# A decoder layer in float32: the sixth pair of up products as seven products of halves, its weight sums kept in DRAM

## The chip, the cores and the metric

One core of a Trainium2 chip runs the whole kernel. The metric is device microseconds of one execution; a kernel is run several times, and the median counts. A profile is taken of one execution more, and its trace gives each instruction's engine, start and length. The engines are PE (matmuls; its weight loads are listed as PEld), DVE and ACT (element by element), POOL, and SP, which here only issues DMAs, in the order in which they stand.

## What is computed

The reference is one post-norm decoder layer on 512 tokens of 1024 features, all in float32: forgetting attention with 16 heads, a gated MLP with a causal convolution over three tokens, and a gated embedding.

```
proj = x @ w_in;  q, k, v, f_logit = split(proj)
c = cumsum(log_sigmoid(f_logit + b_f))
s = q k^T / 8 + c_i - c_j  (causal);  mix = softmax(s) v @ w_out
x = layer_norm(alpha * x + mix)
u, g = split(x @ w_up);  g = causal_dwconv(g, conv_w, conv_b)
x = layer_norm(alpha * x + (gelu(g) * u) @ w_down)
x = x + sigmoid(x @ w_gate + b_gate) * (p @ w_proj)
```

The MLP is 2816 wide: u and g are 22 blocks of 128 features each, and two neighbouring blocks f = 2j, 2j + 1 are a pair j, from 0 to 10.

## The kernel before, in words

**Products.** Every operand is cut in two parts of PE's float32r type, a high part (names ending in h or hi) and the low rest (l or lo), and each product is three matmuls: high by high, high by low, low by high (`three`, line 147). A weight unit is a tile of 128 x 1024 numbers. The class `Weights` (line 64) holds the list of units in the order of their use, loads them from DRAM on SP into four buffers (tag `raw`, `load_to`, line 81; in the MLP every fifth unit goes into a spare tile, `side`), and cuts them (`cut_to`, line 105): ACT writes `whi` (line 123), DVE writes `wlo` (line 129). There are five `whi`/`wlo` buffers, so a unit is cut up to four units before its use, when the product five units back is done.

**Order.** V is projected in three groups of heads (`value_rows`, line 399), the first together with the first Q/K block. Then a loop over h takes head h's scores (`scores`), the projection of a later Q/K block (`project`), the transposes of head h-1's probabilities (`turn`) and head h-2's values (`values`), and at the end the out projection. Here a scheduler decides how the instructions of each engine stand. The MLP follows in four parts of three pairs (the last of two). Each part's up products (`up`, line 763, or `up_step`, line 810) have the down products of the part before laid in (`down`, line 884; chains named x, y, z, added into y by DVE, `add_half`, line 674). From line 945 on the order of DVE and ACT is the order in which the code is written (`manual_schedule`); PE's is still the scheduler's.

**Plain pairs.** `up` makes u or g of one block f as eight chained products of 128 x 512, 24 matmuls. `conv` (line 773) reads g from PSUM, and `product` multiplies with u from PSUM into the tile E.

**Pairs in UP_PAIRS** (line 34). Of the 2 x 2 blocks (two features' blocks by two halves of the 1024 inputs, and two halves of the tokens) seven products of halves are made in place of eight, by Strassen's scheme in Winograd's form. `up_step` does it in four steps, each for g and for u: st 0 makes two products of 128 x 256 per k, st 1 and st 2 two each, st 3 one. Between the steps ACT copies halves of PSUM into E and DVE adds. The weights enter as sums of blocks (`up_units`, line 238). For pairs not kept, DVE makes the sums as the unit is used (`t12`, `t3`, `t4`).

**Kept pairs** (`KEPT`, line 36). Their sums are made early, while DVE has time, and stored in DRAM as an item `kept[j, q]` for each of u and g. An item is made by `keep_load` (line 455: two loads of 512 KB into `ka`, one buffer, and `kb`, one of the four `raw` buffers) and by `keep_sums` (line 469: four subtractions of 128 x 512 on DVE); the next `keep_load` first stores the item (two DMAs) and then loads the next. Before, this is called ahead of V's second group, between the groups, and in the head loop at h = 0 and every even h from 4 to 14.

**Down operands.** The pair's result E (one buffer) becomes the operands of the down products by `operand_sums` (four additions on DVE) and `operand_parts` (names a, b, s with the pair's number, three copies on ACT and three subtractions on DVE). For a pair in `APART` (line 40) this work for the pair before it is written behind the pair's own first step, and E is taken anew after it; else it is written right behind the pair before.

Of the kernel before, what the change touches and what calls it, by code (L numbers as in the profile page):

```python
# [24 lines left out]
KD = D // P  # L25
# [5 lines left out]

CHUNKS = (None, (1,) * 12, (1,) * 12, (2, 1) * 4)

UP_PAIRS = (2, 3, 4, 6, 7, 9)

KEPT = (3, 4, 6, 7)

DMA_PAIRS = (1, 2)

APART = (2, 3, 4, 7)  # L40
HALF = S // 2
ALPHA = 2.0 ** 0.25
EPS = 1e-5
# [99 lines left out]
def trunk_layer(ctx: ExitStack, tc: tile.TileContext, xT, x2d, pT, w0, wqk, wv1, wv2, bf, wo, wup, cwb,  # L143
# [142 lines left out]
    for part in range(4):  # L286
# [3 lines left out]
        for i in range(2 * len(fs)):  # L290
            f, q = fs[i // 2], i % 2
            j, n = f // 2, i % 4
            if j in UP_PAIRS:
                stages = up_units(j)
# [101 lines left out]

    proj = {}

    def value_rows(n):
        h0, nh = V_HEADS[n]  # L400
        w = VF if n == 0 else wv[n].shape[1]
        pv = [bank(f"pv{t}_{n}") for t in range(NT)]
# [3 lines left out]
        for k in range(KD):  # L406
# [21 lines left out]
            if n == 0 and k == 0:  # L428
                with tc.issue_after(cut_first):
                    cut_x(1)  # L430
        for t in range(NT):
            if n == 0:
                logits[t] = fl_all[:, t * H:t * H + H]
                nc.scalar.activation(logits[t], pv[t][:, nh * DH:w], AF.Copy)
            v = V[:, t, h0:h0 + nh]
            p3 = pv[t][:, :nh * DH].rearrange("p (h d) -> p h d", d=DH)
            nc.scalar.activation(v[:, :, 0, :], p3, AF.Copy)
            nc.vector.tensor_sub(v[:, :, 1, :], p3, v[:, :, 0, :].bitcast(F32))
# [30 lines left out]
    def keep_sums():  # L469

        if in_work:
# [9 lines left out]
            behind.close()  # L481
            made.append((to, ab))


    stacks, probs = {}, {}

# [139 lines left out]

    stack(0)
    keep_load()
    value_rows(1)
    stack(1)  # L630
    keep_sums()
    keep_load()
    value_rows(2)
    for h in range(H + 2):
        m, s = divmod(h, 2)
        if h == 2:
            project(2, 0)
        if h < H:
            scores(h)

            if s == 0 and h != 2:
                keep_sums()
                keep_load()
        if m + 1 < KD and h != 2:
            project(m + 1, s)
        for k in OUT_FIRST.get(h, ()):
            out_first(k)
        if s == 1 and h + 1 < H:
            stack(h + 1)
        if 1 <= h < H + 1:  # L650
            turn(h - 1)
        if h >= 2:
            values(h - 2)
        if s == 1 and h + 1 < H:
            stack(h + 2)
        if h == H:
            y = base.tile([P, NT, D], F32, tag="xh", name="y")
            for t in range(NT):
                nc.sync.dma_start(y[:, t, :], x2d[t * P:(t + 1) * P, :])
# [271 lines left out]
    for part in range(4):  # L931
# [7 lines left out]
        for f in range(6 * part, min(6 * part + 6, NF)):  # L939
# [39 lines left out]
            else:  # L979
# [3 lines left out]
                n = 4 * (j - 3 * part) + 2 * q  # L983
# [245 lines left out]
```

## Time and profile before

| | |
|---|---|
| median of 3 runs | 646.31 us (645.73 to 647.5) |
| profiled execution | 646.34 us, its span 644.4 us |
| granted clock of PE | 0.999 |
| busy: PE, DVE, ACT, POOL | 638.1, 532.5, 384.2, 127.8 us |
| HBM read, written | 107.72 MB, 18.87 MB |

The time of an execution holds the span of its trace, from the first to the last instruction, and 1.94 us around it. PE counts as busy from a matmul's start to its modelled end, so its share alone does not tell how fast it goes: the chain that ended last, read in order of time, tells where PE went on and where it waited. The attention with the first half of its out projection takes the first 220 us or so; the MLP's up products run from 247 to 565 us.

### The profile page before, as it was taken

The numbers are of one execution on the slowest core, as the hardware profiler recorded it, in microseconds if no ns is written. First come the engines' busy times: TensorE is split into PE (matmuls) and PEld (weight loads), VectorE is DVE, ScalarE is ACT, GpSimd is POOL, SyncE is SP. The second block draws the span as 40 slices with busy tenths as digits, with TensorE's granted clock in tenths as the row PEclk, the third lists the DMA queues.
The fourth block names the chain that finished last, engine by engine and source line by source line (L and its number), as shares of the span: only waits on it lengthen the run. The fifth ranks groups of instructions, "written<-read, shape, count | busy, mean of one in ns | idle before, by whom it ended". The sixth has DMA issues, their size and how long they took to land.

```text
span 644.4 us, 10100 instructions
## 1 busy us (share of the span) xinstructions
PE 638.1 (99%) x3635; PEld 562.4 (87%) x3635; DVE 532.5 (83%) x866; ACT 384.2 (60%) x685; POOL 127.8 (20%) x147
## 2 busy tenths in 40 slices
PE   8999999999999999999999999999999999999997
PEld 7999888888888889989999988999988998888886
DVE  6674779988888599857899987889797998699997
ACT  6463777877775316945657563647555455336872
POOL 2000554454456043110000010101011001002001
PEclk9999999999999999999999999999999999999999
DMA  8863625454588387684776839665746764772632
GB/s 287 273 213 131 205 83 179 160 187 155 184 263 322 129 257 216 140 213 145 212 221 159 231 121 246 194 206 149 240 132 199 192 217 116 168 272 65 228 109 98
DMA packets 49441, 121.08 MB, mean 188 GB/s; under 512 B 4912, under 2 KB 7984, under 8 KB 49392
## 3 DMA queue, kind: packets, MB, share of 16 engines
q1 hardware_dynamic: 44448, 107.20, 49.8%
q0 software_dynamic: 4800, 13.11, 10.9%
q8 instruction: 28, 0.46, 0.3%
q14 instruction: 21, 0.17, 0.1%
q10 hardware_dynamic: 144, 0.14, 0.1%
HBM read 107.72 MB, written 18.87 MB: 196 GB/s over the span
## 4 chain that ended last, share of the span: by engine, by line
PE 96%; DVE 2%; DMA 1%; issue 0%; ACT 0%; SPq 0%; DVEq 0%
PE g L152 18%; PE u L152 18%; PE pp L152 13%; PE x L152 8%; PE pv L152 7%; PE pl L152 7%; PE z L152 4%; PE r L152 3%; PE ap L152 3%; PE o L581 3%; PE t L568 2%; PE ao L152 2%; PE y L152 2%; PE s L531 2%; PE s L533 2%; PE p L152 1%
## 5 line engine op out<-in xcount | busy, mean ns | idle before, releaser
L123 ACT ACTIVATE whi<-raw 128x1024 fp32r<-128x1024 f32 (+4 forms) x139 | 128.6, 929 | 91.5 <-PE pv L152 15.3
L129 DVE TENSOR_TENSOR wlo<-raw,whi 128x1024 fp32r<-128x1024 f32 (+5 forms) x134 | 140.3, 1055 | 28.3 <-ACT whi L123 27.7
L555 POOL TENSOR_SCALAR pr<-pr,rl 128x128 f32<-128x128 f32 (+1 forms) x64 | 75.5, 1197 | 128.6 <-DVE rl L551 128.6
L281 POOL COPY neghalf<-neghalf 128x1 f32<-128x1 f32 x16 | 9.0, 563 | 247.0 <-ACT neghalf L280 247.0
L152 PE MATMUL g<-x1h,whi 128*128 128x256 f32 (+1 forms) x168 | 54.7, 325 | 0.0
L152 PE MATMUL g<-x1l,whi 128*128 128x256 f32 (+1 forms) x168 | 54.4, 324 | 0.0
L152 PE MATMUL g<-x1h,wlo 128*128 128x256 f32 (+1 forms) x168 | 54.4, 324 | 0.0
L152 PE MATMUL u<-x1l,whi 128*128 128x256 f32 (+1 forms) x160 | 52.9, 331 | 0.0
L152 PE MATMUL u<-x1h,wlo 128*128 128x256 f32 (+1 forms) x160 | 52.9, 331 | 0.0
L152 PE MATMUL u<-x1h,whi 128*128 128x256 f32 (+1 forms) x160 | 52.9, 331 | 0.0
L152 PE MATMUL pp<-xh,wlo 128*128 128x512 f32 (+1 forms) x130 | 50.7, 390 | 0.0
L152 PE MATMUL pp<-xh,whi 128*128 128x512 f32 (+1 forms) x130 | 50.4, 388 | 0.0
L152 PE MATMUL pp<-xl,whi 128*128 128x512 f32 (+1 forms) x130 | 50.4, 387 | 0.0
L547 ACT ACTIVATE pr<-s,nm 128x128 f32<-128x128 f32 (+1 forms) x64 | 33.6, 528 | 9.2 <-DVE nm L543 9.0
L152 PEld LDWEIGHTS g<-x1h,whi 128*128 128x128 f32 x168 | 31.9, 190 | 3.4 <-issue 0.7
L152 PEld LDWEIGHTS g<-x1l,whi 128*128 128x128 f32 x168 | 31.9, 190 | 2.7
L152 PEld LDWEIGHTS g<-x1h,wlo 128*128 128x128 f32 x168 | 31.9, 190 | 2.5
L152 PEld LDWEIGHTS u<-x1h,whi 128*128 128x128 f32 x160 | 30.4, 190 | 3.0
L152 PEld LDWEIGHTS u<-x1l,whi 128*128 128x128 f32 x160 | 30.4, 190 | 3.0
L152 PEld LDWEIGHTS u<-x1h,wlo 128*128 128x128 f32 x160 | 30.4, 190 | 2.8
L123 ACT ACTIVATE whi<-side 128x512 fp32r<-128x512 f32 (+1 forms) x33 | 25.5, 782 | 10.7 <-DVE wlo L129 1.8
L152 PE MATMUL pv<-whi,xh 128*128 128x384 f32 (+1 forms) x96 | 31.0, 322 | 0.7 <-ACT whi L123 0.6
(636 smaller groups left out, 1869.4 us busy)
## 6 DMA issues: line engine op xcount, KB each, us to landing
raw<-wup SPq DMA_DIRECT2D x34, 512.0 KB, 9.6
raw<-wdn SPq DMA_DIRECT2D x23, 512.0 KB, 6.2
raw<-wqk SPq DMA_DIRECT2D x14, 512.0 KB, 4.0
ka<-wup SPq DMA_DIRECT2D x8, 512.0 KB
kb<-wup SPq DMA_DIRECT2D x8, 512.0 KB
kept<-kb SPq DMA_DIRECT2D x8, 512.0 KB, 3.2
kept<-ka SPq DMA_DIRECT2D x8, 512.0 KB
raw<-wo SPq DMA_DIRECT2D x8, 512.0 KB, 4.2
```

The source lines that it names most:

```text
L123: self.nc.scalar.activation(hi[:, c:e], piece, AF.Copy)
L129: self.nc.vector.tensor_sub(lo[:, c:e], piece, hi[:, c:e].bitcast(F32))
L152: nc.tensor.matmul(ps, lhsT, rhs, start=start and n == 0, stop=stop and n == 2, skip_group_check=on)
L281: with tc.issue_after(nc.gpsimd.tensor_copy(small[:, m + 32:m + 33], small[:, m:m + 1]).ins):
L531: nc.tensor.matmul(ps[:, :n], QA[:, q], KA[:, :n], start=True, stop=False)
L533: nc.tensor.matmul(ps[:, :n], qb[0:68, q], kb[0:68, :n], start=False, stop=True)
L547: nc.scalar.activation(pr[:, off:off + w], ps[:, :w], AF.Exp, bias=nm[:, i:i + 1], scale=-1.0, accum_out=ls[:, i:i + 1])
L555: nc.gpsimd.tensor_scalar_mul(pr[:, off:off + w], pr[:, off:off + w], rl[:, i:i + 1])
L568: nc.tensor.transpose(ps[:, w:w + P], pr[:, o:o + P], ident)
L581: nc.tensor.matmul(ps[:, q0:], V[:, j, h], p[:, o:o + w], start=j == 0 and n == 0, stop=j == NT - 1 and n == 1)
```

## The change

The sixth pair (j = 5), plain before, joins `UP_PAIRS` and `KEPT`, so its four plain products become seven products of halves for g and for u, and two more items are kept (ten in place of eight). Pairs 5 and 6 join `APART`. The two more items are made by calls of `keep_sums` and `keep_load` (now together `keep`) in the middle of V's second and of V's third group; the calls in the head loop are as many as before, and each now works on an item two further in the list.

```
-UP_PAIRS = (2, 3, 4, 6, 7, 9)
-KEPT = (3, 4, 6, 7)
+UP_PAIRS = (2, 3, 4, 5, 6, 7, 9)
+KEPT = (3, 4, 5, 6, 7)
...
-APART = (2, 3, 4, 7)
+APART = (2, 3, 4, 5, 6, 7)
...
-    def value_rows(n):
+    def value_rows(n, amid=None):
...
+            if amid is not None and k == KD // 2:
+                amid()
...
+    def keep():
+        keep_sums()
+        keep_load()
...
     stack(0)
     keep_load()
-    value_rows(1)
+    value_rows(1, keep)
     stack(1)
-    keep_sums()
-    keep_load()
-    value_rows(2)
+    keep()
+    value_rows(2, keep)
```

On SP, between V's second group and head 0's scores, the queue of before has the Q/K weights of the first heads (raw18 to raw22; QA1 is a row of the second head's operands) and one load of an item's `kb`:

```order
L511 DMA QA1_573<-QA1_573 64x512
L93 DMA raw18_631<-wqk 128x1024
L93 DMA raw19_661<-wqk 128x1024
L93 DMA raw20_691<-wqk 128x1024
L466 DMA kb4_0_761<-wup 128x1024
L93 DMA raw21_768<-wqk 128x1024
L93 DMA raw22_828<-wqk 128x1024
```

After it, in the same place (kept3_1 and kept4_0 are the second and third items in DRAM):

```order
L93 DMA raw17_613<-wqk 128x1024
L462 DMA kept3_1_64<-kb3_1_532 128x1024
L462 DMA kept3_1_64<-ka3_1_531 128x1024
L93 DMA raw18_643<-wqk 128x1024
L93 DMA raw19_673<-wqk 128x1024
L468 DMA ka4_0_601<-wup 128x1024
L468 DMA kb4_1_694<-wup 128x1024
L93 DMA raw20_713<-wqk 128x1024
L462 DMA kept4_0_65<-kb4_0_602 128x1024
L468 DMA kb5_0_783<-wup 128x1024
L462 DMA kept4_0_65<-ka4_0_601 128x1024
L93 DMA raw21_790<-wqk 128x1024
```

The stores of two items and the loads of two more now stand between the Q/K weights. raw21 takes the buffer that the third item's `kb` had, so its load waits for that item's store; before, it waited for the cut of raw19. On ACT the high part of raw21 is cut ahead of head 0's exponentials, before as after.

On DVE, from the last product of the fifth pair (E4 is its E, a4l and so on the low parts of its down operands, x, y and z the down products' sums), before:

```order
L786 TENSOR_TENSOR E4_3898<-a8_4131,E4_3898 128x512
L873 TENSOR_TENSOR E4_3898<-E4_3898 128x256
L874 TENSOR_TENSOR E4_3898<-E4_3898 128x256
L875 TENSOR_TENSOR E4_3898<-E4_3898 128x256
L876 TENSOR_TENSOR E4_3898<-E4_3898 128x256
L882 TENSOR_TENSOR a4l_4140<-E4_3898,a4h_4139 128x512
L882 TENSOR_TENSOR b4l_4142<-E4_3898,b4h_4141 128x256
L882 TENSOR_TENSOR s4l_4144<-E4_3898,s4h_4143 128x1024
L223 TENSOR_TENSOR raw84_4092<-raw84_4092,side_2724 128x512
L129 TENSOR_TENSOR wlo83_4162<-raw83_4044,whi83_4161 128x1024
L129 TENSOR_TENSOR wlo84_4192<-raw84_4092,whi84_4191 128x512
L679 TENSOR_TENSOR y_2402<-y_2402,x00_3474 128x512
```

And in the change, from the same product (g10 is the sixth pair's g in PSUM, `side` here the place of its first step's half):

```order
L790 TENSOR_TENSOR E4_3920<-a8_4154,E4_3920 128x512
L129 TENSOR_TENSOR wlo83_4173<-raw83_4066,whi83_4172 128x1024
L844 TENSOR_TENSOR side_2746<-g10_4171,side_2746 128x256
L223 TENSOR_TENSOR side_2746<-side_2746 128x512
L129 TENSOR_TENSOR wlo84_4208<-raw84_4114,whi84_4207 128x1024
L683 TENSOR_TENSOR y_2424<-y_2424,x00_3496 128x512
L683 TENSOR_TENSOR y_2424<-y_2424,x01_3497 128x512
L683 TENSOR_TENSOR y_2424<-y_2424,z00_3494 128x512
L683 TENSOR_TENSOR y_2424<-y_2424,z01_3495 128x512
L129 TENSOR_TENSOR wlo85_4231<-side_2746,whi85_4230 128x512
L877 TENSOR_TENSOR E4_3920<-E4_3920 128x256
L878 TENSOR_TENSOR E4_3920<-E4_3920 128x256
```

The fifth pair's sums and low parts have moved behind the sixth pair's first cuts and the four y adds; the two more sums, a join for u, and then a4l, b4l and s4l follow. The sixth pair's new E can be written by ACT only when s4l has been made. On PE the six matmuls of a down product (unit 82) now stand in the middle of the second step's g product, and those of unit 85 behind it.

More of the change, by code (lines that the diff above doesn't have):

```diff
@@ L641, in trunk_layer @@
             if s == 0 and h != 2:
-                keep_sums()
-                keep_load()
+                keep()
         if m + 1 < KD and h != 2:
```

## The prediction

> **What bounds the kernel now.** I read the page first (busy times, then the shares of the chain that ended last), then the chain of waits in order of time around the sixth pair, the busy times by stage, and last the timelines of single engines at the two places the change touches. From the page:
>
> ```profile
> span 644.4 us, 10100 instructions
> PE 638.1 (99%) x3635; PEld 562.4 (87%) x3635; DVE 532.5 (83%) x866; ACT 384.2 (60%) x685; POOL 127.8 (20%) x147
> PE 96%; DVE 2%; DMA 1%; issue 0%; ACT 0%; SPq 0%; DVEq 0%
> ```
>
> PE carries 96% of the chain, so a change pays what it takes off PE less what it makes PE wait. The chain in order of time (start, length, what), from the end of the fifth pair (j = 4) over the sixth (j = 5) to the start of the seventh; the last row is a plain half step of the fifth pair, for comparison:
>
> ```profile
> 373.33 1.44 PE u L152 x12
> 374.77 5.47 PE g L152 x24
> 380.23 1.36 PE x L152 x6
> 381.59 1.36 PE z L152 x6
> 382.95 5.44 PE u L152 x24
> 388.39 2.27 PE x L152 x10
> 390.66 5.69 PE g L152 x24
> 396.35 0.45 PE x L152 x2
> 396.80 5.44 PE u L152 x24
> 402.24 1.36 PE x L152 x6
> ...
> 343.65 2.88 PE g L152 x24
> ```
>
> The four pieces of 24 between 374.77 and 402.24 are the sixth pair's plain products, 128x512 each; the x and z pieces between them are down products that are laid in. No piece is followed by a gap. The second reading is how full DVE is in that stretch (columns: PE, PEld, DVE, ACT, POOL busy, clock, DMA share, GB/s):
>
> ```profile
> 340.77:371.89 31.12, 31.12 (x219) 29.16 (x218) 28.92 (x41) 19.76 (x35) 2.43 (x4) 1.00 0.72 199
> 371.89:403.60 31.71, 31.71 (x153) 26.45 (x152) 25.11 (x37) 16.17 (x25) 3.07 (x4) 1.00 0.66 184
> 403.60:431.84 28.24, 28.24 (x194) 26.28 (x194) 23.76 (x35) 14.81 (x27) 2.91 (x4) 1.00 0.67 198
> ```
>
> A kept pair (first row, j = 4) runs DVE at 93% and PE still never waits; the sixth pair (second row) has been the rest in between, with 6.6 us of DVE free.
>
> **The products themselves.** Removed: 4 x 24 matmuls of 128x512 at 5.44 us per 24, 21.76 us. Added: seven products of halves for u and for g, 3 x 24 + 12 matmuls of 128x256 each, at 2.88 per 24 and 1.44 per 12 (rows at 343.65 and 373.33): 2 x (3 x 2.88 + 1.44) = 20.16. All of it is on the path: -1.60 us. The down products between them stay. One plain piece, at 390.66, takes 5.69 where its like takes 5.44: the third product follows the plain conv of the first, and the 0.25 us goes with the plain form (bounds 0 and -0.25; I take -0.25, since a kept pair has no product that waits for the conv of its own pair's first half).
>
> A page of the Trainium skill speaks on the first term: "TensorE: Matmul & The Clock Gate", section "Wait — 56ns, not 53.3ns?", has back-to-back warm matmuls start N ÷ 2.4 GHz plus about 2.5 ns apart, 109 ns for 256 columns and 216 for 512. By it the pair would fall from 20.7 to 18.4 us, an estimate of -2.4 instead of -1.60. The trace does not agree: 2.88 over 24 is 120 ns and 5.44 over 24 is 227 ns, so here a half costs 53% of a whole, not 51%.
>
> **DVE and ACT in the sixth pair.** A kept pair cuts seven 1024-units' worth of weights where a plain one cuts four, and joins the products on DVE. From the groups of the fifth pair (columns: count, busy, mean ns, idle before):
>
> ```profile
> L129 DVE TENSOR_TENSOR wlo<-raw,whi 128x1024 fp32r<-128x1024 f32 x8 | 9.8, 1222 | 1.2 <-ACT whi L123 1.2
> L129 DVE TENSOR_TENSOR wlo<-raw,whi 128x512 fp32r<-128x512 f32 x3 | 2.0, 690 | 0.4 <-ACT whi L123 0.2
> L851 DVE TENSOR_TENSOR E<-g,E 128x512 f32<-128x512 f32 x1 | 0.7, 693 | 0.4 <-PE g L152 0.4
> L840 DVE TENSOR_TENSOR side<-g,side 128x256 f32<-128x256 f32 x1 | 0.4, 418 | 0.0
> ```
>
> Cuts: 6 x 1.22 + 2 x 0.69 - 4 x 1.22 = 3.82; joins: 2 x 0.42 + 2 x 0.69 = 2.2; 6.0 us more on DVE. Put into the second window that is 25.11 + 6.0 = 31.1 against 31.71 - 1.6 = 30.1 us: DVE overdrawn by 1.0 us there, with 28.24 - 23.76 = 4.5 us free in the next. So PE will wait somewhere in the pair, and the question is how long. The place is the third step: its g product needs two ACT copies into the new E tile, and those wait until DVE has read the last of the old one. The fifth pair shows that chain without a wait (product of the pair before, first cut after it, two y adds, last low part, second copy), and the last row is the sixth pair's own start:
>
> ```profile
> 348.55 0.69 DVE L786 TENSOR_TENSOR E<-a,E 128x512 f32<-128x512 f32 x1 [0.16 <-ACT a L785]
> 356.80 1.22 DVE L882 TENSOR_TENSOR s3l<-E,s3h 128x1024 fp32r<-128x1024 f32 x1
> 358.86 0.37 ACT L845 ACTIVATE E<-g 128x256 f32<-128x256 f32 x1
> 386.56 1.28 DVE L679 TENSOR_TENSOR y<-y,x 128x512 f32<-128x512 f32 x2
> 379.66 0.69 DVE L786 TENSOR_TENSOR E<-a,E 128x512 f32<-128x512 f32 x1 [0.16 <-ACT a L785]
> ```
>
> In the fifth pair the product ends at 349.24, the last low part at 358.02 (8.8 later), the copy at 359.23 (1.2 more). In the sixth the same list has four y adds (2.5) and a 512 cut (0.7) more and a 1024 cut (1.2) less, so 10.8 us: from 380.35 to 391.1, and the copy ends at 392.3. PE arrives there after 4 x 2.88 of halves and 2.72 + 1.36 + 1.36 of down products: 374.77 + 16.96 = 391.73. It waits 0.55 us. The down product before it (the first of those with six matmuls) needs the first y add: 380.35 + 0.1 + 1.22 + 0.42 + 0.69 + 1.22 (cut, join, subtraction, cut) + 0.7 = 384.7, and PE is there at 374.77 + 2.5 x 2.88 + 2.72 = 384.7: nothing to spare, nothing lost. So +0.55, bounds 0 and 2.0 (every link later by the 1.0 us of overdraft, twice). The rest of the overdraft meets the pair's last steps: bounds 0 and +1.0, taken +0.2, nearest to the free 4.5 us behind it. The seventh pair's operands of the sixth are now made in its own first steps, as the eighth pair has it already, plus two ACT copies of 0.4 us with ACT at 14.81 of 28.24: nothing. The pair reads 1.5 MB more by DMA in a stretch at share 0.66; the fifth reads as much at 0.72 and waits for nothing: nothing.
>
> **The two items made beside V.** Each is two loads, four sums, two stores of 512 KB. The sums (all eight items have the same lengths) and the stage they go into:
>
> ```profile
> L477 DVE TENSOR_TENSOR ka<-kb,ka x8: 685/686/692, 25.3 to 194.0; 128x512 f32<-128x512 f32 x8
> 52.00:56.00 4.00, 4.00 (x25) 4.00 (x24) 1.02 (x2) 1.06 (x1) 0.00 (x0) 1.00 0.38 131
> 56.00:60.00 4.00, 4.00 (x25) 4.00 (x24) 1.11 (x2) 1.06 (x1) 0.00 (x0) 1.00 0.37 129
> ```
>
> 2 x 4 x 0.7 = 5.6 us of sums, with 2.9 us of every 4 free on DVE there, and PE never waiting: the sums cost nothing. The transfers are another matter, since SP issues in order and takes them ahead of the later Q/K weights. The rows of that chain (a wqk group from 44.16 holds three issues, one from 57.10 two; then ACT and POOL of head 0, and PE's transposes of it; last the median times to landing):
>
> ```profile
> 42.08 0.96 DVE L129 TENSOR_TENSOR wlo<-raw,whi 128x768 fp32r<-128x768 f32 x1
> 44.16 4.93 SPq L93 DMA_DIRECT2D raw<-wqk  x3
> 57.10 4.44 SPq L93 DMA_DIRECT2D raw<-wqk  x2
> 63.06 1.05 ACT L123 ACTIVATE whi<-raw 128x1024 fp32r<-128x1024 f32 x1
> 64.51 1.28 ACT L547 ACT_TABLE_LOAD   x1
> 65.81 0.37 ACT L547 ACTIVATE pr<-s,nm 128x128 f32<-128x128 f32 x1
> 67.74 0.21 ACT L547 ACTIVATION_READ_ACCUMULATOR pr<-s,nm 128x1 f32 x1
> 68.27 4.81 POOL L555 TENSOR_SCALAR pr<-pr,rl 128x128 f32<-128x128 f32 x4 [63.41 <-DVE rl L551]
> 76.52 1.25 PE L568 MATMUL t<-ident,pr 128*128 128x128 f32 x10
> raw<-wqk SPq DMA_DIRECT2D x14, 512.0 KB, 4.0
> kept<-kb SPq DMA_DIRECT2D x8, 512.0 KB, 3.2
> ```
>
> The load of raw21 goes out at 57.10 now. In the change it takes the buffer of the third item's kb, so it waits for that item's store: the second item's last sum ends at about 42.08 + 2.8 (sums) + 0.7 + 2 x 0.95 (what stands between them) = 47.5; its store lands 3.2 later, 50.7; the third item's load takes 4.0 and, behind five other transfers of 512 KB, about 1.5 more, 56.2; three sums, 58.3; store 3.2, 61.5; then raw21, 4.0 and some queueing, about 66. The high part of raw21 is cut on ACT ahead of head 0's exponentials, and from its landing it is 1.05 + 1.3 + 2.1 + 0.3 + 4.8 = 9.6 us to the last scaled row, which PE needs at about 76.5. So the landing may be as late as 66.9 before PE waits; beyond that every us costs one. I take +0.2, bounds 0 and +5 (below). A gain is excluded: PE has no gap there to close.
>
> **Sum.** -1.60 - 0.25 + 0.55 + 0.2 + 0.2 = -0.9 us on the profiled execution's 646.34 (span 644.4 and 1.94 around it), which stands at the median of the runs, 646.31: 645.4.
>
> **Rivals.** (1) The chain of transfers beside V decides: four legs stand in a row (store, load, store, load), and if each takes 1.5 us more than I gave it, raw21 lands near 72 and PE stands 5 us at head 0's transposes: 650.5, slower. For it: only 0.9 us are to spare, and the stage's bytes double (4 MB more in some 30 us, beside 130 GB/s). Against it: the same legs land in 3.2 to 4.0 us today. It decides from a landing at 66.9. (2) DVE's overdraft costs more than 0.75 us, each of three waits (y add, copy, last step) 0.7 to 1 us: about +2.0 in place of 0.75 and nothing gained, 646.3 to 647.5. For it: 93% in the pair before and no rest in between. Against it: the 4.5 us behind. (3) No wait at all: 646.34 - 1.85 = 644.5. For it: PE shows no wait in the kept pair before it. (4) A product of halves costs half a whole: 24 in 2.72 us, the pair in 19.04, -2.72 in place of -1.60: 644.3. The rows at 343.65 and 373.33 speak against it, since they are that very product in the pair before. By the page of the Trainium skill named above it would be 644.6, an estimate. That the products are not made as said is excluded: the changed program has 72 matmuls more on PE, 168 for 96.
>
> **Chances.** About 0.3% of this kernel, 1.94 us, is what a measurement of it can tell from no change: faster is below 644.4, slower above 648.25. Forecast (644.9 to 646.2) 0.43, all within. Rival 2: 0.22, of it 0.02 slower. Rival 3: 0.20, of it 0.11 faster, since it sits on the bound and the runs shown spread by 0.6 below their median. Rival 1: 0.13, of it 0.11 slower. Rival 4: 0.02, faster. That makes 0.13 faster, 0.74 within, 0.13 slower. The range reaches down to rival 3 less 0.4 of that spread, 644.1, and up into rival 1, 648.9, which leaves out some 0.07 below and 0.08 above.
>
> **What would show it.** In the profile after: 24 matmuls of 128x256 in 2.88 us all through the pair, 168 of them; a wait of PE of about half a us at the third step, released by ACT's copy; DVE near 100% in the stretch of the sixth pair and freer in the seventh; head 0's exponentials starting 1.5 to 3 us later against the scores, and its transposes still at 76.5. The forecast is wrong if head 0's transposes move, if the pair from 374.77 takes more than 28.8 us, or if PE's time changes in the attention or behind the seventh pair.

## The result, and the profile after

The changed kernel takes 650.71 us (median of 9 runs, 648.54 to 653.61) against 646.55 us (median of 9, 645.73 to 647.5): 1.0064 of the time, 95% interval 1.0045 to 1.0084. The forecast of 645.4 is wrong in sign, and the time lies above the range. It is close to the 650.5 of the first rival, and the experiments show that rival's chain of transfers at work; they also show that the pair itself gains nothing (1.0011 of the time with the pair alone). The profiled execution took 652.2 us. Its page:

```profile
span 650.3 us, 10314 instructions
PE 638.8 (98%) x3707; PEld 564.9 (87%) x3707; DVE 542.5 (83%) x882; ACT 391.2 (60%) x703; POOL 127.8 (20%) x147
PE 80%; DMA 7%; DVE 7%; ACT 2%; issue 2%; POOL 1%; SPq 0%; DVEq 0%; ACTq 0%
```

PE's share of the chain fell from 96% to 80%; DMA and DVE hold 7% each. PE's busy time rose by only 0.7 us (638.1 to 638.8) where the span rose by 5.9 (644.4 to 650.3). So the time came as waits, and the chain says where. First the stage beside V and head 0, in order of time (start, length, what):

```profile
47.71 4.82 DMA kept<-ka
...
52.54 6.83 DMA ka<-wup
...
61.67 2.90 DMA kept<-kb
...
64.58 5.69 DMA raw<-wqk
...
70.35 1.06 ACT whi L123
...
71.43 1.28 ACT L553
...
72.72 2.16 ACT pr L553 x8
...
75.19 4.93 POOL pr L561 x4
...
80.16 0.98 PE t L574 x7
```

These are the legs of the prediction's chain, store, load, store, load, and then the cut of unit 21 (the cut at 70.35), the exponentials, the scaling and the transposes of head 0. Each leg is in the place where it was expected, and three of the four are longer. PE's waits in this stage, from its timeline:

```profile
65.03 0.50 PE L152 MATMUL pp<-xh,wlo 128*128 128x512 f32 x1 [0.61 <-DVE V L440]
...
73.23 0.50 PE L537 MATMUL s<-KA,QA 128*128 128x512 f32 x1 [1.80 <-ACT pr L553]
...
90.37 0.50 PE L587 MATMUL o<-PTh,V 128*128 128x512 f32 x1 [1.35 <-ACT pr L553]
```

The same product of head 0 with V in the kernel before:

```profile
85.38 0.50 PE L581 MATMUL o<-PTh,V 128*128 128x512 f32 x1
```

It starts 5.0 us late now, and 5.4 us of lateness reach the sixth pair. The first of the three waits is for V's last rows, which DVE adds behind the third item's sums, and those waited for their load. The second, 1.80 us, is for head 0's exponentials, at head 1's scores; at head 0's transposes themselves PE waits only 0.22 us more. In the sixth pair the chain reads:

```profile
395.05 0.92 DVE s4l L886
...
396.19 0.83 DVE wlo L129
...
397.32 0.68 DVE raw L223
...
399.06 0.69 DVE wlo L129
...
399.77 8.35 DMA raw<-wup
...
408.22 0.04 ACT whi L123
...
409.18 0.37 ACT E L859
...
409.60 2.41 PE g L152 x18
```

DVE ends the operand parts of the pair before at 396, then cuts weights that have been waiting for it. Only with these cuts do buffers come free, so the load that PE will need leaves at 399.77. It lands 8.35 us later; ACT cuts that unit and only then copies a finished result out of PSUM, and PE, which needs that bank for the seventh pair's first product, has waited 1.27 us.

In the table, which serves all the experiments too, the three columns behind the ratio are read from each profiled execution's timeline: the start of head 0's product with V, the start of the sixth pair, and the time from there to the start of the ninth (three pairs). Where nothing was changed ahead of it, the first of these columns lies between 85.2 and 85.9, which is its spread; `exps_h1_ordered`'s profiled execution is an exception, since it lost some 3 us at its start, with half the clock between 10 and 14 us.

| kernel | median us | ratio, 95% interval | head 0 x V | sixth pair | three pairs |
|---|---|---|---|---|---|
| before | 646.55 | 1 | 85.38 | 374.60 | 91.07 |
| changed | 650.71 | 1.0064, 1.0045 to 1.0084 | 90.37 | 380.00 | 91.93 |
| items_only | 650.48 | 1.0056, 1.0044 to 1.0069 | 88.63 | 378.03 | 91.05 |
| pair_only | 647.24 | 1.0011, 1.0002 to 1.0019 | 85.90 | 375.21 | 91.44 |
| small_transfers | 648.40 | 1.0030, 1.0020 to 1.0040 | 87.06 | 376.73 | 92.38 |
| no_sums | 650.54 | 1.0052, 1.0032 to 1.0071 | 87.74 | 377.38 | 93.40 |
| exps_first | 647.39 | 1.0018, 1.0005 to 1.0030 | 85.74 | 375.10 | 91.10 |
| exps_h1 | 647.09 | 1.0011, 1.0000 to 1.0022 | 85.92 | 375.20 | 91.30 |
| heads_items | 656.09 | 1.0131, 1.0110 to 1.0153 | 85.39 | 382.10 | 91.34 |
| heads_pool | 660.33 | 1.0218, 1.0204 to 1.0232 | 85.69 | 388.69 | 92.35 |
| late_items | 651.62 | 1.0079, 1.0065 to 1.0092 | 85.88 | 380.89 | 91.06 |
| late_ordered | 654.12 | 1.0106, 1.0082 to 1.0130 | 85.42 | 383.38 | 91.76 |
| copies_first | 650.57 | 1.0061, 1.0047 to 1.0075 | 89.75 | 379.13 | 91.19 |
| pair_relief | 645.06 | 0.9981, 0.9972 to 0.9989 | 85.72 | 374.98 | 90.19 |
| pair_ordered | 646.70 | 1.0007, 0.9996 to 1.0018 | 85.21 | 374.52 | 91.78 |
| exps_pool | 651.13 | 1.0069, 1.0052 to 1.0087 | 87.81 | 377.08 | 93.92 |
| exps_pool_h1 | 649.39 | 1.0052, 1.0035 to 1.0070 | 84.77 | 374.59 | 93.92 |
| exps_h1_ordered | 647.11 | 0.9999, 0.9988 to 1.0011 | 88.38 | 377.61 | 91.61 |

The ratio is against the runs of the kernel before on the same chip, whose medians lay between 646.33 and 646.62. It need not equal the quotient of the medians; the intervals decide.

### The profile page after: what moved, and what is told of

Its sections match the earlier page's. It is cut to its first block, busy times and chain, and to the rows that moved or that the text cites. A ratio compares the mean times of both kernels' runs of the same rounds, so it can differ in the third digit from the quotient of the medians.

```text
span 650.3 us, 10314 instructions
## 1 busy us (share of the span) xinstructions
PE 638.8 (98%) x3707; PEld 564.9 (87%) x3707; DVE 542.5 (83%) x882; ACT 391.2 (60%) x703; POOL 127.8 (20%) x147
## 4 chain that ended last, share of the span: by engine, by line
PE 80%; DMA 7%; DVE 7%; ACT 2%; issue 2%; POOL 1%; SPq 0%; DVEq 0%; ACTq 0%
PE g L152 16%; PE u L152 16%; PE pp L152 10%; PE x L152 7%; PE pl L152 7%; PE z L152 4%; PE r L152 3%; PE ap L152 3%; PE o L587 3%; PE ao L152 2%; PE t L574 2%; PE y L152 2%; PE s L537 1%; DVE wlo L129 1%; PE s L539 1%
## 5 line engine op out<-in xcount | busy, mean ns | idle before, releaser
L123 ACT ACTIVATE whi<-raw 128x1024 fp32r<-128x1024 f32 (+4 forms) x142 | 131.1, 929 | 101.2 <-DMA raw<-wqk 17.7
L129 DVE TENSOR_TENSOR wlo<-raw,whi 128x1024 fp32r<-128x1024 f32 (+5 forms) x137 | 143.5, 1055 | 27.8 <-ACT whi L123 27.0
L561 POOL TENSOR_SCALAR pr<-pr,rl 128x128 f32<-128x128 f32 (+1 forms) x64 | 75.7, 1200 | 133.6 <-DVE rl L557 133.6
L152 PE MATMUL g<-x1h,whi 128*128 128x256 f32 (+1 forms) x164 | 51.8, 316 | 1.3 <-ACT E L859 1.3
L152 PE MATMUL g<-x1l,whi 128*128 128x256 f32 (+1 forms) x164 | 51.6, 315 | 0.0
L152 PE MATMUL g<-x1h,wlo 128*128 128x256 f32 (+1 forms) x164 | 51.5, 314 | 0.0
L152 PE MATMUL u<-x1h,whi 128*128 128x256 f32 (+1 forms) x156 | 50.1, 321 | 0.3 <-DVE E L855 0.3
L152 PE MATMUL u<-x1l,whi 128*128 128x256 f32 (+1 forms) x156 | 50.1, 321 | 0.0
L152 PE MATMUL u<-x1h,wlo 128*128 128x256 f32 (+1 forms) x156 | 50.1, 321 | 0.0
L152 PE MATMUL g<-xsh,whi 128*128 128x256 f32 x112 | 31.7, 283 | 0.1
L152 PE MATMUL u<-xsl,whi 128*128 128x256 f32 x112 | 31.7, 283 | 0.0
```

What stands on the lines that cost most here:

```text
L123: self.nc.scalar.activation(hi[:, c:e], piece, AF.Copy)
L129: self.nc.vector.tensor_sub(lo[:, c:e], piece, hi[:, c:e].bitcast(F32))
L152: nc.tensor.matmul(ps, lhsT, rhs, start=start and n == 0, stop=stop and n == 2, skip_group_check=on)
L561: nc.gpsimd.tensor_scalar_mul(pr[:, off:off + w], pr[:, off:off + w], rl[:, i:i + 1])
```

## The experiments

Theory 1: the two items beside V cost nearly all of it, since their transfers make a weight unit late and head 0's softmax waits for that. Theory 2: the pair's products save what was forecast, and waits in the pair give it back. The rivals stand with each run.

### The two halves of the change, each alone

`items_only` takes the pair out and leaves the items; `pair_only` leaves the pair and makes no item for it.

```diff
 items_only, against the changed kernel
-UP_PAIRS = (2, 3, 4, 5, 6, 7, 9)
+UP_PAIRS = (2, 3, 4, 6, 7, 9)
-APART = (2, 3, 4, 5, 6, 7)
+APART = (2, 3, 4, 7)
 pair_only, against the changed kernel
+    kept.update({(5, q): kept[4, q] for q in range(2)})
-    value_rows(1, keep)
+    value_rows(1)
-    value_rows(2, keep)
+    value_rows(2)
```

> The changed kernel with the sixth pair's products as they were before (whole halves, 192 of its 128x512 matmuls back), and the two more items still made beside V; what they keep is never read. Theory 1 (the items' transfers make the seventh weight piece of the second head pair land some 4 us late, so head 0's softmax and transposes come late): head 0's transposes start at 80 to 82 us in place of 76.5, everything behind stays 3 to 5 us late, 649.5 to 651.5. Rival A (the items are hidden, and the sixth pair's seven products cost it all): transposes at 76.5, 646.2 to 646.9.

> The changed kernel with nothing made beside V's second and third groups: the sixth pair still runs as seven products, but reads the kept sums of the pair before it, so its output is not the reference's; sizes, queues and order in the pair stay. Theory 1 with theory 2 (in the pair the products save 1.85 us, and waits at its end give 2.2 back): head 0's transposes at 76.5, the pair takes 29.0 to 29.5 us against 28.83, 646.6 to 647.5. Rival B (the waits at the pair's end came only of the late phase in which the pair ran, so the products' gain stays): the pair takes 27.0 to 27.6 us, 644.6 to 645.2. Rival A: 650 or more.

The items alone give 1.0056, with the three pairs at 91.05 as before: 3.6 us by the ratio. The pair alone gives 1.0011: 0.7 us. Together 4.3 us, for 4.1 of the whole change. Rival A (all of it is the pair) and rival B (the products' gain stays) are out. Head 0's transposes in `items_only` start at 77.53, not at 80 to 82, though the product behind them is 3.3 us late: that marker was too narrow.

### By which queue the items cost time

`small_transfers` loads and stores a quarter of the second and third item, with VectorE's long sums kept; `no_sums` keeps the transfers and leaves those sums out.

```diff
 small_transfers
-                nc.sync.dma_start(t.rearrange("p (a b) -> p a b", b=P), wup[2 * j + n, 1 - q])
+                w = 4 if len(to_keep) in few else 1
+                nc.sync.dma_start(t.rearrange("p (a b) -> p a b", b=P)[:, ::w, :], wup[2 * j + n, 1 - q][:, ::w])
...
 no_sums
+            if len(to_keep) not in (7, 8):
                 nc.vector.tensor_sub(b11, b12, b11)
...
```

> The changed kernel with the loads and stores of the second and third item a quarter as large; their order, queue and buffers, and VectorE's four 128x512 sums for each stay (written to a spare tile, with four small ones behind them). Pairs that would read these two read other kept items, so the output is not the reference's. Theory 1 (the transfers' time makes the weights of head pair 1 late): head 0's transposes at 76.5 to 77.5, 646.7 to 647.8. Rival E (VectorE's 5.5 us of sums beside V and their place in the queues make it late, whatever the bytes): transposes at 79 us or later, 649.5 to 651.

> The changed kernel without VectorE's four sums for the second and third item; both are loaded and stored unsummed, so the pairs that read them compute something else. Against the run with small transfers it says what VectorE's part is. Theory 1 (mostly the transfers, for which the small ones gave back 2.3 of the 4.2 us): the stores leave up to 2 us sooner, head 0's transposes at 78.5 to 80.5, 649 to 650.4. Rival E (VectorE's sums weigh as much): 647.5 to 648.5.

Head 0's product starts 3.3 us sooner with small transfers and 2.6 us sooner without the sums. Neither alone brings back the 5.0 us, and neither expectation was met cleanly: the bytes and the sums are links of one chain (load, sums, store, next load), and shortening either helps in part. The median of `no_sums` stayed at 650.54 all the same. Its profiled execution lost the gain again in the pairs (93.40 for three), at a wait of 1.79 us that was followed by some us at half the clock (last section). Its six runs part by the mean granted clock: 647.41 and 648.06 us at 1.000 and 0.999, 650.01 to 651.48 us at 0.996 and 0.997. So that median holds a loss by the clock beside what the items cost.

In the trace of the changed kernel the thing that hands the lateness on to PE is ACT's order: the cut at 70.35 stands ahead of the exponentials at 72.72, while head 0's reductions had ended on DVE at 68.2. Unit 21 belongs to the fourth Q/K block, which is not projected before the fifth head. `exps_first` puts the cuts of units 21 and 22 behind the exponentials of heads 0 and 1; nothing else.

```diff
             behind = ExitStack()
+            if self.cut in self.after:
+                behind.enter_context(self.tc.issue_after(self.after[self.cut]))
...
-            nc.scalar.activation(pr[:, off:off + w], ps[:, :w], AF.Exp, ...
+            last = nc.scalar.activation(pr[:, off:off + w], ps[:, :w], AF.Exp, ...
+            if h < 2:
+                W.after[21 + h] = last
```

> The changed kernel with one order fixed: ScalarE cuts the weight units 21 and 22 behind the exponentials of head 0 and head 1 in place of ahead of or among them; everything is computed. Theory 1 in its narrow form (it is the cut of unit 21, waiting for its late load, that stands on ScalarE ahead of head 0's exponentials, while unit 21 itself is needed only some 20 us later): the exponentials start at 67 to 69 in place of 72.7 us, TensorE's wait of 1.8 us at head 1's scores is gone; what is left is VectorE's lateness (head 0's reductions at 66.3 against 63.7, head 1's behind an item's sums that wait for its load), so head 0's product with V starts at 87 to 89 us against 85.4 and 90.4, and the time is 647.8 to 649.3. Rival E (the transfers hold up VectorE and everything behind it as well): product at 90 or later, 650 or more.

That is 1.0018 for 1.0064: two cuts in another place in ACT's row bring back about 3 us. ACT's timeline of it:

```profile
64.52 0.37 ACT L555 ACTIVATE pr<-s,nm 128x128 f32<-128x128 f32 x1
...
67.93 1.06 ACT L125 ACTIVATE whi<-raw 128x1024 fp32r<-128x1024 f32 x1 [1.08 <-DMA raw<-wqk]
...
74.65 0.37 ACT L555 ACTIVATE pr<-s,nm 128x128 f32<-128x128 f32 x1 [4.00 <-DVE nm L551]
```

The exponentials of head 0 start at 64.5 in place of 72.7, and the cut waits for its load with nobody behind it. Even the load comes sooner, 67.9 in place of 70.3. Head 0's product with V starts at 85.74, and the time lies below both ranges that were given. The last row is what is left: head 1's exponentials wait for DVE, whose reductions of head 1 stand behind the fourth item's sums, and these wait for that item's load. PE still waits 0.59 us in front of 85.74. `exps_h1` moves that item's sums behind head 1's scores.

```diff
-            if s == 0 and h != 2:
+            if s == 0 and h not in (0, 2) or h == 1:
```

> Everything is computed: the items beside V as in the change, ScalarE's cuts of units 21 and 22 behind the exponentials, the fourth item's sums behind head 1's scores, nothing moved to GpSimd, the pairs as in the change. Theory 1 (in the run with GpSimd the second half of wo started at 219.0 us against 219.6 before, so the items cost nothing in this order): the items are free, what is left is the price of the pair, 646.4 to 647.2. Rival D (VectorE's sums ahead of head 2's keys): a wait at head 2's scores, 648 or more.

1.0011, the number of the pair alone, with head 0's product and the sixth pair within 0.1 us of it. So in this order the two items beside V cost nothing that can be measured, and PE's timeline has no wait between 60 and 110 us. What the second move is worth by itself is not shown, since the intervals of `exps_first` and `exps_h1` overlap. Theory 1 is borne out in a narrower form: the transfers were late as its chain said, but they cost time through two engines' orders, ACT's cut ahead of the exponentials and DVE's sums ahead of the reductions.

### The items in other places

`heads_items` makes them in heads 5 and 9, `late_items` behind the last head's scores, `heads_pool` in heads 5 and 9 with their sums on POOL (and both changes of order in the pairs, below).

```diff
 heads_items
-            if s == 0 and h != 2:
+            if s == 0 and h != 2 or h in (5, 9):
 late_items
+        if h >= H:
+            keep()
 heads_pool, on top of heads_items
+            eng = nc.gpsimd if len(to_keep) in (6, 3) else nc.vector
```

> The changed kernel with the two items made in heads 5 and 9 of the attention in place of beside V; everything is computed. Theory 1: head 0's transposes back at 76.5, and since VectorE and the transfers have room there (15.7 to 16.4 of 18 us busy, transfers 0.5), TensorE stays without a gap between 94 and 202 us: the time is that of the kernel without the items, 646.6 to 647.5. Rival D (VectorE has no room in those heads either: 2.8 us of sums in each of the two heads push the reductions of an odd head, which stand behind them): 2 to 5 us of waits in heads 5 and 9, 649 to 652.

> The changed kernel with nothing made beside V: the items keep their order, and the ninth and tenth are made behind the last head's scores, where VectorE was busy 8.9 of 18 us; everything is computed. Theory 1: head 0's transposes at 76.5, no new gap of TensorE between 200 and 240 us, so what is left is the price of the pair alone, 646.9 to 647.5. Rival F (the first rows and the second half of wo come in there too, transfers 0.96 busy between 184 and 202 us, and are pushed back by the items): TensorE waits 1 to 3 us between 200 and 240 us, 648 to 650.

> Everything is computed: the two items in heads 5 and 9, but their four sums on GpSimd (its 128x512 scaling took 1.6 us, so 6.4 us for each item, where GpSimd is busy 9 of 18 us), and the two changes of order in the pairs. Theory (in heads 5 and 9 it was VectorE's place in the row that cost, not the transfers): TensorE without a wait over 0.5 us in the heads, 645.0 to 646.0, below both kernels. Rival J (GpSimd's sums stand ahead of the scaling of the next head's probabilities, or slow VectorE's own instructions beside them): waits of 1 to 3 us for GpSimd or VectorE in heads 6 and 10, 647 to 650.

All three cost more than the places beside V. My expectation, made from DVE's busy share, fell each time, and each time lies above the rival's range too. The chain of `heads_items` through heads 5 to 7:

```profile
119.61 2.73 DMA kept<-ka
122.36 4.17 DMA ka<-wup
...
131.40 0.69 DVE ka L482
...
132.12 0.30 DVE s L549
...
135.70 0.69 DVE KA L524
...
136.44 0.50 PE s L537 x2
```

The items share one buffer. From the store of head 5's item to the end of the sums of head 6's it takes 12.5 us (119.6 to 132.1), and a head takes 9; with an item in each of heads 4, 5 and 6 the last sums come so late that head 7's reductions, which the code orders behind them, and the low part of the next keys behind those make PE wait (1.80 us in front of 136.44). With the sums on POOL head 5's item holds the buffer longer, and PE's wait near the same place (at 135.41), for exponentials behind the same reductions, is 2.85 us; four heads later it is 2.85 us again (at 179.26). Not all of the cost is waiting. Behind these waits the clock fell: 0.54 and 0.61 between 138 and 142 us in `heads_items`, 0.50 from 136 to 142 and from 180 to 186 us in `heads_pool`. By the missing clock that is an estimated 1.7 us in the first and some 5.7 us in the second, out of the 7.5 and 14.1 us by which their sixth pairs start late. In `late_items` it is again a load that blocks DVE's row; DVE, then PE:

```profile
224.29 0.69 DVE L479 TENSOR_TENSOR ka<-kb,ka 128x512 f32<-128x512 f32 x1 [2.64 <-DMA ka<-wup]
224.90 0.68 DVE L597 TENSOR_TENSOR ol<-o,oh 128x512 fp32r<-128x512 f32 x1
```

```profile
225.64 0.50 PE L152 MATMUL ao<-whi,ol 128*128 128x512 f32 x1 [2.07 <-DVE ol L597]
```

The last item's sum waits 2.64 us for its load, and the low part of the last heads' output, which PE needs next, stands behind it. It was not DVE's busy time that started the loss in any of the places, it was what stood behind a wait.

### The pair

`copies_first` lets ACT copy the pair's last results out of PSUM ahead of the next cuts; `pair_relief` is `pair_only` without the low parts of units 86 and 87 (PE reads the high parts twice), 2.4 us of DVE's work less; `pair_ordered` is `pair_only` with the copies first and, in the seventh pair, the sum that frees up's bank ahead of the four operand sums.

```diff
 copies_first (up_step)
-        hi, lo = W.get(u_up[j, st, s], 4)
+        late = j == 5 and st == 3
+        hi, lo = W.parts[u_up[j, st, s]] if late else W.get(u_up[j, st, s], 4)
...
             nc.scalar.activation(e[:, HALF:S], x, AF.Copy)
+            if late:
+                W.get(u_up[j, st, s], 4)
 pair_relief (cut_to)
+                elif self.cut in (86, 87):
+                    lo = hi
 pair_ordered (up_step), beside copies_first's
-            if amid is not None:
+            if amid is not None and j != 6:
                 amid()
             nc.vector.tensor_add(c1 if j in APART else e[:, :HALF], x, c1)
+            if amid is not None and j == 6:
+                amid()
```

> The changed kernel with one thing moved: at the sixth pair's last step ScalarE copies the finished results out of PSUM first and cuts the next weights afterwards. Theory 2 (the seventh pair's first product waits for a PSUM bank whose copy stands on ScalarE behind a cut that waits for a late load): TensorE's wait there falls from 1.4 us to 0.3 or less, 649.4 to 649.8 where the changed kernel has 650.7. Rival C (the late load itself is what TensorE needs next, so the wait only moves to the next product): no change, 650.7, with a wait of about 1 us released by the cut of the seventh pair's second weights.

> The kernel with the pair alone (nothing made beside V, the pair reads another pair's kept sums), and with the low parts of the weight units 86 and 87 not made (TensorE reads the high parts twice, so the products are not the reference's): 2.4 us less for VectorE in the middle of the sixth pair, which is what frees the buffers of the loads behind. Theory 2 as a chain (VectorE late by its 4 us of operand sums and parts, so buffers are freed late and in a burst, so the next loads land late, so ScalarE and TensorE wait): the waits of 0.63 and 0.75 us at the pair's end fall to 0.4 or less in all, 645.5 to 646.1. Rival H (the loads land late because the transfers are at their rate there, 300 to 405 GB/s, however early they are issued): the waits stay, 646.9 to 647.3.

> The pair alone (nothing made beside V, the pair reads another pair's kept sums) with the two changes of order: the copies out of PSUM ahead of the cuts at the sixth pair's last step, and in the seventh pair the sum that frees up's bank ahead of the four sums of operands. Theory 2: each wait hangs on an operation that was only queued behind work that could be later, so the pair's waits go but for 0.3 us at the third step, 645.0 to 645.7 against 647.2 in the order of the change. Rival G (VectorE has too much work there, something else is late): 646.6 or more.

`copies_first` takes the wait of 1.27 us away: the pair lasts 27.65 us (379.13 to 406.78), 1.19 less than before. But the time does not fall (1.0061), for a wait of much the same length, 1.02 us, turns up in the seventh pair, in its chain:

```profile
399.92 9.19 DMA raw<-wdn
...
421.28 0.42 DVE E L883
...
421.70 0.35 DVE side L845
...
422.09 1.94 PE u L152 x14
```

The next late load, 9.19 us from issue to landing, now starts the chain, DVE does its work behind it without a break, and PE waits for a sum on DVE. Rival C named the right effect and the wrong place. With that order mended too (`pair_ordered`) the sixth pair takes 27.65 us, but the seventh and the eighth take 0.65 and 1.24 us more than before, with a wait of 0.67 us for a y add in the eighth (at 452.08); three pairs take 91.78, and the interval of its ratio and that of `pair_only` overlap. Rival G stands: whatever goes first, something else is late. Taking work off DVE is another matter (`pair_relief`):

```profile
392.52 3.14 PE g L154 x24
395.66 2.88 PE u L154 x24
398.54 1.39 PE x L154 x6
399.93 1.43 PE g L154 x12
401.36 1.44 PE u L154 x12
...
402.83 3.14 PE g L154 x24
```

PE's timeline shows no wait at the pair's end or behind it, and the ratio is 0.9981 against 1.0011 for the same kernel with the two low parts: 1.9 us for 2.4 us of DVE's work. Rival H (the transfers' rate sets it) is out, since the same loads go out there, most of them 0.6 to 2.4 us sooner. So the pair's products do gain, and two cuts on DVE in the middle of the sixth pair, 2.4 us of its work, cost PE nearly as much. This kernel leaves out a part of the result, so it is a measurement and not a way to have the gain.

### Everything computed, with the orders mended

`late_ordered` is `late_items` with both changes of order in the pairs. `exps_pool` is `exps_first` with the low parts of units 86 and 87 on POOL, which is idle there; `exps_pool_h1` has the fourth item's sums moved as well. `exps_h1_ordered` is `exps_h1` with the two orders of the pairs and nothing on POOL.

```diff
 exps_pool (cut_to)
+                    eng = self.nc.gpsimd if self.cut in (86, 87) else self.nc.vector
-                    self.nc.vector.tensor_sub(lo[:, c:e], piece, hi[:, c:e].bitcast(F32))
+                    eng.tensor_sub(lo[:, c:e], piece, hi[:, c:e].bitcast(F32))
```

> The same with two changes of order: the copies ahead of the cuts at the sixth pair's last step, and in the seventh pair VectorE's sum that frees up's bank ahead of the four sums of operands. Theory 2 as it stands after the run with the copies first (each wait is an operation that TensorE waits for, behind work on ScalarE or VectorE that could be later): both waits are gone, the pairs keep the products' gain but for 0.3 us, 645.0 to 645.9. Rival G (VectorE has too much work from the sixth pair on, and whatever is put first, something else is late): a wait of 0.7 to 1.5 us at a third place, 646.6 to 647.5.

> The same, and in the sixth pair GpSimd makes the low parts of the units 86 and 87 in place of VectorE (its 128x512 scaling took 1.6 us, so some 3.2 us for 128x1024; it is idle there); everything is computed. Theory 2 (2.4 us of VectorE's work too much in the pair, as the run without these low parts showed): the pair and the one behind it together take 90.0 to 90.6 us against 91.9, and the time is 1.0 to 1.8 us below the run with the exponentials first, 646.2 to 647.9. Rival K (GpSimd's low parts come later than TensorE needs them, or VectorE slows beside GpSimd): no gain, or up to 2 us more.

> The same, and the fourth item's sums and the store and load behind them stand behind head 1's scores in place of head 0's, so head 1's reductions no longer wait for that item's load; everything is computed. Theory 1: head 0's product with V at 86 to 87 us, 645.2 to 646.6, about the kernel before or a little below it. Rival D (as in heads 5 and 9: VectorE's sums now stand ahead of the low part of the next head's keys): a wait of 1.5 to 3 us at head 2's scores, 648 or more.

> The same with the two changes of order in the pairs (copies ahead of the cuts, the sum that frees up's bank ahead of the four operand sums). Rival G, which the pair alone in this order bore out (646.7 against 647.2: waits gone in two places and back by 0.8 us in a third): 0.3 to 0.6 us less than without them, 645.9 to 646.8, within 0.3% of the kernel before. Theory 2 in its first form (the products' gain comes through once no wait is left in the sixth pair): 644.6 to 645.5.

`late_ordered` lost more at the end of the attention than `late_items` (its wait for the last low part was 3.90 us for 2.07), and its three pairs took 91.76. `exps_pool` and `exps_pool_h1` lost 2.9 us in the pairs (93.92): DVE stood still beside POOL, below. The front half of `exps_pool_h1` showed the fourth item's place to be right, which led to `exps_h1`. None of the four met the range that was hoped for. The first two lie above their rivals' ranges as well; `exps_pool_h1` lies in its rival's, but the wait that this rival named, at head 2's scores, is not there. `exps_h1_ordered` comes out at 0.9999, interval 0.9988 to 1.0011: the change can be had at no loss that these runs show. Its median is that of `exps_h1` (647.11 and 647.09) and the intervals overlap, so a gain from the two orders is not shown. No version with everything computed was faster than the kernel before.

## Why the prediction was wrong, point by point

- **-1.60 for the products: right.** The chain of `pair_relief` has 24 matmuls of 128x256 in 2.88 us, and PE has 3707 instructions for 3635. Where neither order nor DVE holds it up (`copies_first`, `late_items`), the pair lasts 27.65 us for 28.84, -1.19; forecast was -1.60 - 0.25 + 0.55 = -1.30. The plain piece's 0.25 was not tried by itself. (168 steps of 109 ns are 18.3 us, not 18.4; the estimate of -2.4 stands.)
- **+0.55 at the third step: right in place and nature, too large.** The matmul at 397.54 in the changed kernel starts 0.29 us late, behind ACT's two copies.
- **+0.2 for the rest of DVE's overdraft: failed, and the overdraft itself was misread.** PE's waits at the pair's end were 0.30 and 1.27 us in the changed kernel, 0.48 and 0.59 in `pair_only`; the bound given was 1.0. (These are idle times of the timeline. Against an even step of 0.12 us each start is 0.16 us later still, and the expectations of the runs count so.) The sum put 6.0 us more on DVE into the sixth pair. The windows of the sixth and the seventh pair, before and in the changed kernel, say otherwise (columns as in the prediction):

```profile
374.60:403.43 28.83, 28.83 (x128) 23.59 (x127) 23.31 (x34) 14.18 (x22) 3.07 (x4) 1.00 0.65 177
403.43:434.55 31.12, 31.12 (x217) 29.15 (x216) 26.11 (x38) 17.14 (x30) 2.91 (x4) 1.00 0.67 202
```

```profile
380.00:409.60 29.60, 27.91 (x200) 25.84 (x199) 23.44 (x35) 17.80 (x33) 2.48 (x4) 1.00 0.68 209
409.60:440.81 31.21, 31.21 (x217) 29.25 (x217) 30.30 (x44) 20.61 (x37) 2.43 (x4) 1.00 0.73 207
```

DVE is busy 23.44 of 29.60 us in the sixth pair, hardly more than before, and 30.30 of 31.21 in the seventh: the reverse of the sign that was named, near 100% and then freer. The cuts and joins came in, but the pair's own convolution and gate products, about 4.4 us on DVE, moved out behind its last step. So the free 4.5 us behind were not there. What held PE up was the order inside the pair: late cuts free buffers late, six loads leave within 4 us (397.4 to 401.4), the one that matters lands 8.35 us later, DVE itself stands still 2.73 us for a cut on ACT, and ACT's copies stand behind the cuts that wait for the loads. "Nothing" for the pair's extra loads was read from a mean share of 0.72; it hid the burst (1.00 between 402.0 and 409.6 us).
- **+0.2 for the transfers beside V: failed, and it is most of the miss.** The chain was right link by link, but too short: the second item's last sum ends at 47.69 (47.5 forecast), the store lands at 52.52 (50.7), the load at 59.37 (56.2), three sums 61.65 (58.3), the store 64.56 (61.5), raw21 70.27 (66). Legs of 3.2, 5.5, 3.2 and 4.5 us were 4.8, 6.8, 2.9 and 5.7. The threshold of 66.9 held too: 3.4 us too late at landing, and head 0's transposes end 3.4 us late (81.14 for 77.77). But PE paid most of that ahead of them, at head 1's scores, and head 0's exponentials start 6.9 us later (72.72 for 65.81), not 1.5 to 3. Then came a wait that was not in the sum, 1.35 us at head 0's product. On DVE the fourth item's sums (75.08 to 78.4) stand ahead of head 1's reductions, and on ACT another cut (at 88.32) stands ahead of head 2's exponentials, for which PE waits. In the chain of `items_only` the one leads to the other: late reductions, a late row of head operands on SP, and behind it on SP the load of the unit that this cut waits for. All this cost 3.6 us by `items_only`, where the sum had 0.2.
- **The sums cost nothing: failed in part.** DVE had the time, but the sums are links between a load and a store, so their length counts in the chain (head 0's product 2.6 us sooner in `no_sums`).
- **Rival 1 at 0.13: the choice that failed.** It gave 650.5, and its chain is the one that decided. With 0.9 us to spare on a chain of four transfers whose durations were medians over the whole kernel, and bounds of 0 and +5, a landing behind the threshold was the likelier case: between 40 and 60 us the DMA engines moved 242 GB/s, for 161 before. That its total came within 0.3 us of the measured time is in part luck, since it had 5.2 us for the items and -1.1 for the pair where the runs have 3.6 and +0.7.

## What to carry to other kernels

A transfer that is added beside a full stage is priced by what stands behind its consumer in an in-order queue, and not by the bytes alone: look for the cut, sum or copy that will wait for it, and move what is urgent ahead of that instruction. Here two cuts and four sums in another place brought back what the items cost. And a saving on PE that brings another engine new work is a trade even where that engine is not full over the stage: DVE was busy 83% of the sixth pair in `pair_only`, 2.4 us less for it gave 1.9 us, and mending single waits only moved them.

## What the runs showed of the hardware

**DVE can stand still beside POOL.** In `exps_pool`, POOL's subtraction and DVE's beside it (their timelines):

```profile
393.07 2.51 POOL L132 TENSOR_TENSOR wlo<-raw,whi 128x1024 fp32r<-128x1024 f32 x1 [9.40 <-ACT neghalf L283]
```

```profile
393.27 2.87 DVE L226 TENSOR_TENSOR raw<-raw,side 128x512 f32<-128x512 f32 x1
```

DVE's 128x512 subtraction takes 0.68 us elsewhere and took 2.87 us here, until 0.56 us after POOL was done. The Trainium skill has the reason, in "SBUF — State Buffer", section "Who interferes with whom": a DVE instruction with two SBUF inputs contends with a GpSimd instruction that reads SBUF, for a shared pair of ports that is an exclusive lock. The trace agrees: 2.2 us lost, for the remaining 2.3 us of POOL's instruction. It is not so beside every instruction of POOL: beside its scaling of the probabilities (L561, from 75.19 to 80.12 in the changed kernel) DVE's four sums took 0.69, 0.74, 0.85 and 0.97 us.

**A wait of about 2 us can halve the clock for some us after.** PE alone in `late_items` behind its wait of 2.07 us (columns: length of the stretch, PE busy, granted clock, DMA share, GB/s):

```profile
226.00:228.00 2.00, 2.00 (x9) 0.79 0.04 8
228.00:230.00 2.00, 2.00 (x6) 0.50 0.75 309
230.00:232.00 2.00, 2.00 (x9) 0.85 0.64 238
```

The same in `no_sums` behind a wait of 1.79 us:

```profile
406.00:408.00 2.00, 1.02 (x6) 0.84 1.00 360
408.00:410.00 2.00, 2.00 (x11) 0.50 0.86 297
410.00:412.00 2.00, 2.00 (x14) 0.81 0.73 243
```

By the missing clock the first cost 0.21 x 2 + 0.50 x 2 + 0.15 x 2 = 1.7 us of PE's work on top of the wait. The waits of 1.80 us in the changed kernel's profile (at 73.23) and of 2.12 us in `exps_pool` (at 408.66) were followed by none of it, though a wait of the same 1.80 us in `heads_items` (at 136.44) was. The Trainium skill, "TensorE: Matmul & The Clock Gate", section "What's actually happening", gives an idle window of about 3.4 us that runs freely as the condition for half the clock. That it depends on where a wait falls agrees with these runs; that a wait of 1.79 us can be enough is what they add. It may be part of the wide spread of the changed kernel's runs: its slowest, 653.61 us, had a mean clock of 0.995 where the others had 0.999 or 1.000. There is no trace of that run, so this is not shown.
